# Norm vectors spread by TensorE, expert retrieval for two heads at a time, side work billed by VectorE time, gMLP first in the mixer

## The chip, the cores and the metric

The kernel runs on one core of a Trainium2 chip. The metric is the device time of one execution in microseconds (us); lower is better. The five engines named here are TensorE (PE), VectorE (DVE), ScalarE (ACT), GpSimd (POOL) and SyncE (SP). SP issues the plain transfers, POOL the indirect ones.

## The reference

Two layers act on 256 tokens of width 1024 (two blocks of 128 tokens, b = 0 and 1). An input layer norm comes first. Each layer has a mixer and a channel mixer:

```python
mix = _mixer(h, ...)                     # one projection in, GLA heads | gMLP gate, one projection out
h = _layer_norm(ALPHA * h + mix, ln1_g, ln1_b)
ffn = _peer(h, wq, k1, k2, u_tab, v_tab)
h = _layer_norm(ALPHA * h + ffn, ln2_g, ln2_b)
```

The GLA half is gated linear attention in four heads, in chunks of 64, then an RMS norm and a multiplication by `silu(r)`. The gMLP half is `u * (W LN(v) + b)` with `u` and `v` after a gelu, the layer norm having its own two vectors of 512. `_peer` takes, for each token and each of 8 heads, the best 16 of 128 scores in two halves, then the best 16 of the sums of the two, which name 16 experts out of 16384. Each of the 128 chosen experts of a token (8 heads times 16) adds `gate * gelu(u_e . x) * v_e`; `u_e` and `v_e` are rows of 1024 floats.

## The kernel before, in words

**The main loop** (L785 to L811). There are four passes of K = 128 iterations: layer 0 block 0, layer 0 block 1, layer 1 block 0, layer 1 block 1. In an iteration POOL gathers for one expert slot the `u` and `v` rows of 128 tokens (L730, 128 rows of 8 KB, 1.05 MB), DVE forms the dot products with `h` (`dot`, L737), ACT turns them into a diagonal matrix (`weigh`, L743 to L746), and PE adds the weighted `v` rows to two accumulators (L795). Seven buffers `uv` hold gathered rows (UVBUFS), and gathers are issued up to five ahead (AHEAD). A buffer is free for the next gather when its L795 products are done.

**The side work.** While the experts of one block are gathered, the other block is prepared: generator `side` (L752) runs the residual and norm (`residual_block`, `norm_rest`), the mixer (`front`, L281) and the queries (`ask`, L688). It advances at every `yield`. In each iteration `debt` grows by PACE (0.7, 0.64, 0.64, 0.5 by pass) and one step is run for each whole unit (L807 to L811), so a step counts 1 whatever it costs. What is left of a side at the end of its pass is run at once (L803). Program order on PE, ACT and DVE is the order written; SP and POOL take their work as the scheduler sets it.

**The weights.** `front` and `ask` take 45 chunks of 512 KB for each block and layer through `Feed` (L48): SP loads a chunk into one of four buffers `raw`, ACT makes its high part (`split_hi`, L127), DVE the low part (`split_lo`, L132), PE multiplies by both.

**The mixer.** `front` projects the gates, keys and queries (5 chunks), then runs `attention()` and `tokens()` side by side in rounds (L482). `tokens()` projects v, r, sv and su, four chunks each. Only after both have ended come gelu of su, the spatial gate (L488 to L507), and the output projection over 8 chunks (`out`, L494).

**The queries.** `ask` works in rounds: each round starts one of 16 queries (two for each head) and moves the earlier ones a step: projection, copy, sum, product with the keys, copy, `top16` (L603). After the eighth query of a group of HH = 4 heads, `retrieve` (L626) picks the experts of the four heads in six further steps. Before the main loop the whole of block 0's input norm and `front` runs, then rounds of `ask` until the first four heads are retrieved (L777); the rest of `ask` belongs to the first side.

**The norm vectors.** `load_vec` (L167) has SP load a vector of 1024 floats from HBM into all 128 partitions (512 KB) in one of two buffers `vec`; the gMLP vectors `lnv` use the same two buffers (L286). The constants `iota` are loaded into a `raw` buffer (L578).

Of the kernel before, what the change touches and what calls it, by code (L numbers as in the profile page):

```python
# [37 lines left out]
VECS = 2  # L38
PACE = (0.7, 0.64, 0.64, 0.5)
HH = 4  # L40
KH = HH * TK

# [43 lines left out]

class Trunk:
    def __init__(self, ctx, tc, a, dbg=None):
# [11 lines left out]
        nc.sync.dma_start(self.h[:, 0], a["x"][0:128, :])  # L100
        self.ident = cp.tile([128, 128], F32, name="ident")
# [59 lines left out]
    def layer_norm(self, y, g, b):  # L161
        nc = self.nc
        mv, rs = self.norm_stats(y)
        nc.vector.scalar_tensor_tensor(y, y, mv[:, 0:1], g, op0=OP.subtract, op1=OP.mult)
        nc.vector.scalar_tensor_tensor(y, y, rs, b, op0=OP.mult, op1=OP.add)

    def load_vec(self, vec, pool):  # L167
        r = pool.tile([128, D], F32, name="vec", tag="vec", bufs=VECS)
        self.nc.sync.dma_start(r, vec.to_broadcast([128, D]))
        return r  # L170

    def transpose_quarter(self, src, q, xh, xl, later):
# [3 lines left out]
        for i in range(4):  # L176
            dc = q * 4 + i
            nc.tensor.transpose(p[:, i * 128:(i + 1) * 128], src[:, dc * 128:(dc + 1) * 128], self.ident)
# [5 lines left out]
    def wide(self, b, hi, lo):  # L184


        p = self.bank("a")
        v = p[:, :256].rearrange("p (e t) -> p e t", e=2)
# [14 lines left out]
    def norm_sub(self, b, nm, g):  # L203

        for hf in range(2):
            w = slice(hf * 512, (hf + 1) * 512)
            y = self.h[:, b, w]
            self.nc.vector.scalar_tensor_tensor(y, y, nm, g[:, w], op0=OP.add, op1=OP.mult)

    def norm_scale(self, b, hf, rs, be, out, later):  # L210

        nc = self.nc
        w = slice(hf * 512, (hf + 1) * 512)
        y = self.h[:, b, w]
        nc.vector.scalar_tensor_tensor(y, y, rs, be[:, w], op0=OP.mult, op1=OP.add)
        if out is None:
            self.transpose_quarter(self.h[:, b], hf, self.xh[:, b], self.xl[:, b], later)
        else:
            nc.sync.dma_start(out[b * 128:(b + 1) * 128, w], y)

# [5 lines left out]
    def norm_rest(self, b, nm, var, g, be, out):  # L226

        rs = self.pow_half(var)
        self.norm_sub(b, nm, g)
        later = []  # L230
        for hf in range(2):
            self.norm_scale(b, hf, rs, be, out, later)
        for f in later:
            f()

    def bn_norm(self, b, st, g, be, out=None):
# [8 lines left out]
        self.norm_rest(b, nm, t, g, be, out)  # L245
# [35 lines left out]
    def front(self, pp, l, b, feed):  # L281
# [55 lines left out]
        def in_turn(*works):  # L337
# [3 lines left out]
            while works or live:  # L341
# [7 lines left out]
                yield  # L349
# [10 lines left out]
        def attention():  # L360
# [81 lines left out]
            cat, state["uu"] = m2[:, :D], m2[:, D:D + 512]  # L442
            state["cat"] = cat
# [14 lines left out]

        def tokens():
            def bank():  # L460
# [5 lines left out]
                return p  # L466
            p = yield from bank()
            nc.scalar.copy(vv[:, b], p)
            p = yield from bank()
# [3 lines left out]
            p = yield from bank()  # L473
            nc.vector.tensor_tensor(srh, srh, f["gg"].unsqueeze(1).to_broadcast([128, H, 128]), op=OP.mult)
            state["sr"] = sr
            vn = state["vn"] = tile_of("vn", [128, 512])
            nc.scalar.activation(vn, p, AF.Gelu)
            p = yield from bank()
            self.layer_norm(vn, lnv[:, 0], lnv[:, 1])
            state["su"] = p  # L480

        yield from together(attention(), tokens())  # L482
        cat, uu, vn = state["cat"], state["uu"], state["vn"]
        nc.scalar.activation(uu, state["su"], AF.Gelu)
        p = self.bank("b")
        for g in range(4):
            gs = slice(g * 128, (g + 1) * 128)
            nc.tensor.matmul(p[:, gs], lhsT=f["sw"][:, g], rhs=vn[:, gs], start=True, stop=True)  # L488

        g = self.load_vec(a["ln1_g"][l:l + 1], pp)  # L490
        be = self.load_vec(a["ln1_b"][l:l + 1], pp)
        banks = [self.bank("a") for _ in range(2)]

        def out(dc):  # L494
            hi, lo = feed.get()
            for hf in range(2):
                w = slice(hf * 512, (hf + 1) * 512)
                self.mm(banks[hf], [(ch[:, dc], hi[:, w]), (cl[:, dc], hi[:, w]), (ch[:, dc], lo[:, w])], dc == 0,
                        dc == DC - 1)
            feed.split()  # L500
        out(0)
        yield
        for g4 in range(4):
# [3 lines left out]
        out(1)  # L507
        yield
        later = []
        self.transpose_quarter(cat, 1, ch, cl, later)  # L510
        out(2)
        yield
        for w in later:
# [383 lines left out]
```

## Time and profile before

| | us |
|---|---|
| median of 3 runs (1686.33 to 1688.66) | 1688.13 |
| the profiled execution's own time | 1688.3 |
| its span, first to last instruction | 1686.3 |
| DVE busy | 1169.9 |
| PE busy (pipelined, ends modelled) | 1375.3 |
| ACT busy | 772.0 |
| POOL busy | 622.5 |

All rows of the trace are from the profiled execution. A row with "idle before <- X" says how long the engine stood still ahead of that instruction, and what ended it. The transfer rate in a stretch (GB/s) counts all queues. Some instructions overlap the one behind them on the same engine, so the distance between two starts can be a little shorter than the duration.

### The profile page before, as it was taken

How to read it: one execution, taken by the hardware profiler on the slowest of the kernel's cores; microseconds unless marked ns; L12 is line 12 of the kernel's file. 1: busy time of each engine (PE TensorE's matmuls, PEld its weight loads, DVE VectorE, ACT ScalarE, POOL GpSimd, SP SyncE). 2: the span in 40 equal slices, each digit the busy share in tenths (PEclk: the TensorE clock that was granted, in tenths of full speed). 3: DMA queues.
4: the chain of work that ended last, by engine and by line, in shares of the span. 5: the costliest groups of instructions: out<-in, count | busy, mean ns of one | idle time of the engine just before them, and what ended most of it. 6: DMA issues, size and time to landing. Idle time of an engine off the chain costs nothing.

```text
span 1686.3 us, 17419 instructions
## 1 busy us (share of the span) xinstructions
PE 1375.3 (82%) x4448; PEld 727.5 (43%) x4448; DVE 1169.9 (69%) x2638; ACT 772.0 (46%) x2077; POOL 622.5 (37%) x542
## 2 busy tenths in 40 slices
PE   5875699988978798888977799987987877777775
PEld 4764255545633355444643255543652322222221
DVE  4878877666997667666898567766799554444444
ACT  4642376444534466444534456644444333333332
POOL 0001443434335433543335344343334433333331
PEclk9986999998999999998999999999998999999998
DMA  7764999999999999999999999999999999999995
GB/s 261 239 200 146 421 404 418 418 416 419 418 343 402 406 419 418 419 418 419 418 358 390 418 413 418 419 419 419 418 364 351 422 400 421 421 422 421 421 422 240
DMA packets 106406, 649.09 MB, mean 385 GB/s; under 512 B 12066, under 2 KB 12868, under 8 KB 40772
## 3 DMA queue, kind: packets, MB, share of 16 engines
q0 software_dynamic: 73872, 537.49, 77.7%
q1 hardware_dynamic: 32436, 110.50, 17.4%
q8 instruction: 36, 0.59, 0.1%
q14 instruction: 62, 0.51, 0.1%
HBM read 646.90 MB, written 1.05 MB: 384 GB/s over the span
## 4 chain that ended last, share of the span: by engine, by line
DMA 23%; issue 21%; DVE 17%; PE 16%; POOL 13%; ACT 2%; POOLq 1%; DVEq 0%
DMA uv<-uv,eid 23%; POOL uv L730 13%; PE bank_acc L795 9%; DVE junk L737 6%; PE bank_a L138 5%; DVE i L609 1%; DVE wlo L132 1%; DVE v L607 1%; POOLq L730 1%; DVE S L612 1%; DVE pos L609 1%; DVE qp L701 1%; DVE sums L656 1%; ACT whi L127 0%; DVE sc L607 0%
## 5 line engine op out<-in xcount | busy, mean ns | idle before, releaser
L795 PE MATMUL bank_acc<-uv,dg 128*128 128x512 f32 x2048 | 1006.7, 627 | 195.8 <-ACT dg L746 177.2
L730 POOL DMA_INDIRECT uv<-uv,eid x512 | 603.9, 1179 | 922.0 <-PE bank_acc L795 612.4
L737 DVE SCALAR_TENSOR_TENSOR junk<-uv,h 128x1024 f32<-128x1024 f32 x512 | 626.7, 1224 | 440.4 <-DMA uv<-uv,eid 437.2
L795 PEld LDWEIGHTS bank_acc<-uv,dg 128*128 128x128 f32 x2048 | 377.6, 197 | 722.9 <-ACT dg L746 378.6
L743 ACT ACTIVATE dots<-dots 128x1 f32<-128x1 f32 x512 | 103.6, 202 | 656.3 <-DVE junk L737 655.3
L132 DVE TENSOR_TENSOR wlo<-raw,whi 128x1024 fp32r<-128x1024 f32 x180 | 219.2, 1220 | 22.6 <-issue 11.0
L746 ACT ACTIVATE dg<-ident,dots 128x128 f32<-128x128 f32 x512 | 205.6, 402 | 21.8 <-PE bank_acc L795 5.3
L127 ACT CAST whi<-raw 128x1024 fp32r<-128x1024 f32 x180 | 187.3, 1043 | 40.8 <-DMA raw<-wmix 30.4
L744 ACT ACTIVATE dots<-dots,ex 128x1 f32<-128x1 f32 x512 | 150.8, 294 | 16.6
L138 PE MATMUL bank_a<-x,whi 128*128 128x256 f32 x672 | 114.3, 316 | 49.7 <-DVE qp L701 34.5
L138 PE MATMUL bank_a<-whi,x 128*128 128x512 f32 x384 | 134.5, 458 | 1.0 <-ACT whi L127 0.6
L138 PEld LDWEIGHTS bank_a<-x,whi 128*128 128x128 f32 x672 | 93.6, 205 | 71.5 <-DVE qp L701 45.4
L138 PE MATMUL bank_a<-x,wlo 128*128 128x128 f32 x672 | 92.7, 285 | 0.0
L138 PEld LDWEIGHTS bank_a<-x,wlo 128*128 128x128 f32 x672 | 90.9, 209 | 0.0
L138 PEld LDWEIGHTS bank_a<-whi,x 128*128 128x128 f32 x384 | 72.5, 192 | 37.6 <-issue 25.4
L138 PE MATMUL bank_a<-wlo,x 128*128 128x512 f32 x192 | 66.8, 402 | 7.8 <-DVE wlo L132 7.6
L698 ACT COPY f_half<-bank_a 128x128 f32<-128x128 f32 x64 | 16.9, 264 | 69.5 <-PE bank_a L138 60.2
L138 PEld LDWEIGHTS bank_a<-wlo,x 128*128 128x128 f32 x192 | 36.1, 190 | 20.7 <-DVE wlo L132 13.0
L737 DVE DVE_READ_ACCUMULATOR junk<-uv,h 128x1 f32 x512 | 42.1, 82 | 0.0
L704 PEld LDWEIGHTS bank_b<-kt,qp 128*128 128x128 f32 x128 | 24.1, 202 | 39.0 <-issue 21.5
L704 PE MATMUL bank_b<-kt,qp 128*128 128x128 f32 x128 | 27.6, 300 | 14.4 <-DVE qp L701 14.4
L607 DVE MAX8 v<-S 128x8 f32<-128x128 f32 x128 | 37.2, 291 | 2.2
(132 smaller groups left out, 630.5 us busy)
## 6 DMA issues: line engine op xcount, KB each, us to landing
raw<-wmix SPq DMA_DIRECT2D x180, 512.0 KB
uv<-uv,eid POOLq DMA_INDIRECT x512
vec<-ln_g SPq DMA_DIRECT2D x8, 512.0 KB
vec<-ln_b SPq DMA_DIRECT2D x8, 512.0 KB
h<-x SPq DMA_DIRECT2D x2, 512.0 KB
vec<-ln_in_g SPq DMA_DIRECT2D x2, 512.0 KB
vec<-ln_in_b SPq DMA_DIRECT2D x2, 512.0 KB
lnv<-sgu_ln_g SPq DMA_DIRECT2D x4, 256.0 KB
```

Of the source, the lines that this page charges most:

```text
L127: self.nc.scalar.copy(hi, raw)
L132: self.nc.vector.tensor_tensor(lo, raw, hi.bitcast(F32), op=OP.subtract)
L138: self.nc.tensor.matmul(out, lhsT=l, rhs=r, start=start and i == 0, stop=stop and i == n - 1)
L607: nc.vector.max(v[:, r], vals)
L609: nc.vector.max_index(i[:, r], v[:, r], vals)
L704: nc.tensor.matmul(p2, lhsT=q, rhs=kt[:, l, i % 2], start=True, stop=True)
L730: nc.gpsimd.indirect_dma_start(out=uv, out_offset=None, in_=a["uv"], in_offset=bass.IndirectOffsetOnAxis(ap=eid[:, k:k + 1], axis=0), boun ...
L737: nc.vector.scalar_tensor_tensor(junk, uv[:, :D], 1.0, self.h[:, b], op0=OP.mult, op1=OP.mult, accum_out=dots[:, k:k + 1])
L743: nc.scalar.activation(c, c, AF.Gelu)
L744: nc.scalar.mul(c, c, ex[:, k:k + 1])
L746: nc.scalar.mul(dg, self.ident, c)
L795: nc.tensor.matmul(acc[hf], lhsT=dgs[m], rhs=uvs[m][:, D + hf * 512:D + (hf + 1) * 512], start=m % K == 0, stop=m % K == K - 1)
```

## The change

- **Vectors.** One table `vecs` of 16 rows (64 KB) holds all norm vectors and is loaded once. `spread` multiplies a column of the identity, broadcast to 128 columns, with half a row of the table on PE, and so puts that half row on all 128 partitions of a PSUM bank "b". `norm_rest` and the gMLP norm read it there. `load_vec`, `lnv` and the two buffers go.
- **Heads.** HH is 2: `retrieve` runs four times per `ask`, for two heads each, in four steps. The main loop starts once the first two heads are retrieved.
- **Pacing.** Each `yield` names a cost (2.9 for a round of `ask`, 2.3 for a round of attention and tokens, 2.0, 1.3, 1.5 and so on elsewhere, 1.5 where none is named). PACE is 1.65, 1.36, 1.36, 1.5 by pass, and steps are run while `debt` is above 0.
- **Mixer.** `tokens()` takes sv and su first, then v and r. The spatial gate runs beside the later projections (`beside`), and the first half of the output projection (the gMLP rows, OUTS) beside the end of attention.
- **Queries.** Two queries share one PSUM bank "a".
- **Loads.** `iota` gets a tile of its own and comes last of the constants; `x` of block 1 is loaded inside the first side.

```diff
-VECS = 2
-PACE = (0.7, 0.64, 0.64, 0.5)
-HH = 4
+PACE = (1.65, 1.36, 1.36, 1.5)
+OUTS = (4, 5, 6, 7, 0, 1, 2, 3)
+HH = 2
+V_IN, V_LN1, V_LN2, V_SGU, V_LAYER = 0, 2, 4, 6, 5
+def beside(work, other):
+    while True:
+        try:
+            next(work)
+        except StopIteration as e:
+            return e.value
+        next(other, None)
+        yield
         nc.sync.dma_start(self.h[:, 0], a["x"][0:128, :])
+        self.vecs = cp.tile([16, D], F32, name="vecs")
+        nc.sync.dma_start(self.vecs, a["vecs"])
-    def load_vec(self, vec, pool):
-        r = pool.tile([128, D], F32, name="vec", tag="vec", bufs=VECS)
-        self.nc.sync.dma_start(r, vec.to_broadcast([128, D]))
-        return r
+    def spread(self, row, hf=0):
+        p = self.bank("b")
+        self.nc.tensor.matmul(p, lhsT=self.ident[0:16, row:row + 1].to_broadcast([16, 128]),
+                              rhs=self.vecs[:, hf * 512:(hf + 1) * 512], start=True, stop=True)
+        return p
+    def norm_rest(self, b, nm, var, row, out=None):
         rs = self.pow_half(var)
+        gs = [self.spread(row, hf) for hf in range(2)]
+        bs = []
+        y = [self.h[:, b, hf * 512:(hf + 1) * 512] for hf in range(2)]
+        for hf in range(2):
+            nc.vector.scalar_tensor_tensor(y[hf], y[hf], nm, gs[hf], op0=OP.add, op1=OP.mult)
+            bs.append(self.spread(row + 1, hf))
+        yield 1.5
...
-        order += [c + k for c in (C_V, C_R, C_SV, C_SU) for k in range(4)] + [C_OUT + k for k in range(8)]
+        order += [c + k for c in (C_SV, C_SU, C_V, C_R) for k in range(4)] + [C_OUT + k for k in OUTS]
-        lnv = pp.tile([128, 2, 512], F32, name="lnv", tag="vec", bufs=VECS)
-        nc.sync.dma_start(lnv[:, 0], a["sgu_ln_g"][l:l + 1].to_broadcast([128, 512]))
-        nc.sync.dma_start(lnv[:, 1], a["sgu_ln_b"][l:l + 1].to_broadcast([128, 512]))
+            def gating():
+                mv, rs = self.norm_stats(vn)
+                g, be = [self.spread(V_SGU + V_LAYER * l, x) for x in range(2)]
+                yield
+                nc.vector.scalar_tensor_tensor(vn, vn, mv[:, 0:1], g, op0=OP.subtract, op1=OP.mult)
+                nc.vector.scalar_tensor_tensor(vn, vn, rs, be, op0=OP.mult, op1=OP.add)
+                yield
...
+            yield from beside(out(OUTS[:4]), gate)
         yield from together(attention(), tokens())
+        yield from out(OUTS[4:])
+        yield from self.residual_block(banks, b, V_LN1 + V_LAYER * l)
-            r = self.raw()
-            nc.sync.dma_start(r[:, :160], a["iota"])
...
+            r = tile_of("numbers", [128, 160])
+            nc.sync.dma_start(r, a["iota"])
-                yield
-                for h in range(0, HH, 2):
-                    top16(*[(cand[:, x], sc[:, x], pos[:, x]) for x in (h, h + 1)])
-                    yield
+                top16(*[(cand[:, h], sc[:, h], pos[:, h]) for h in range(HH)])
+                yield 2.2
...
                 def query(i):
-                    p = self.wide(b, *feed.get())
+                    if i % 2 == 0:
+                        banks[0] = self.bank("a")
+                    p = self.wide(b, *feed.get(), banks[0][:, i % 2 * 256:(i % 2 + 1) * 256])
...
                     yield from asked
+                    nc.sync.dma_start(self.h[:, 1], a["x"][128:256, :])
                     feed = self.feed_of(0)
+                    yield 0.1
...
                         debt += PACE[min(i // K, 3)]
-                        while debt >= 1:
-                            debt -= 1
-                            if next(work, work) is work:
+                        while debt > 0:
+                            c = next(work, work)
+                            if c is work:
                                 break
+                            debt -= c or 1.5
```

## Rows read from the trace of the kernel before

**Rows 1.** The page: all transfers, and the transfer rate in 40 equal slices.

```profile
DMA packets 106406, 649.09 MB, mean 385 GB/s; under 512 B 12066, under 2 KB 12868, under 8 KB 40772
GB/s 261 239 200 146 421 404 418 418 416 419 418 343 402 406 419 418 419 418 419 418 358 390 418 413 418 419 419 419 418 364 351 422 400 421 421 422 421 421 422 240
```

**Rows 2.** Stretches: window, length, busy us by engine (instructions), PE clock, DMA share, GB/s.

```profile
0.00:157.50 157.50, 108.37 (x594) 94.44 (x594) 118.21 (x306) 75.16 (x127) 6.03 (x16) 0.87 0.61 204
465.00:545.00 80.00, 63.61 (x161) 27.91 (x162) 68.25 (x218) 32.88 (x100) 35.01 (x30) 0.96 0.95 370
855.00:905.00 50.00, 38.63 (x113) 18.43 (x111) 48.07 (x191) 19.47 (x59) 21.67 (x17) 0.97 0.91 341
1240.00:1295.00 55.00, 44.42 (x136) 22.04 (x134) 53.01 (x209) 21.52 (x69) 21.43 (x19) 0.94 0.86 324
1380.00:1655.00 275.00, 217.03 (x438) 73.82 (x436) 135.68 (x220) 98.62 (x330) 107.67 (x109) 1.00 1.01 422
```

**Rows 3.** The transfers of the norm vectors: issues and size.

```profile
vec<-ln_g SPq DMA_DIRECT2D x8, 512.0 KB
lnv<-sgu_ln_g SPq DMA_DIRECT2D x4, 256.0 KB
```

**Rows 4.** Timeline of SP's queue at the start: start, duration, line, transfer.

```profile
15.00 0.33 SPq L579 DMA_DIRECT2D raw<-iota  x1
...
19.81 13.54 SPq L122 DMA_DIRECT2D raw<-wmix  x6
...
70.24 0.33 SPq L169 DMA_DIRECT2D vec<-ln_b  x1
```

**Rows 5.** Timeline of ACT at the start, with idle time before.

```profile
12.67 1.04 ACT L127 CAST whi<-raw 128x1024 fp32r<-128x1024 f32 x1 [10.65 <-DMA raw<-wmix]
...
71.81 0.59 ACT L181 CAST x<-bank_b 128x512 fp32r<-128x512 f32 x1 [4.63 <-PE bank_b L178]
```

**Rows 6.** Timeline of DVE before the first gather.

```profile
10.20 1.41 DVE L208 SCALAR_TENSOR_TENSOR h<-h,nm,vec 128x512 f32<-128x512 f32 x2 [4.20 <-DMA vec<-ln_in_g]
...
108.64 0.29 DVE L607 MAX8 v<-S 128x8 f32<-128x128 f32 x1
...
111.67 0.28 DVE L607 MAX8 v<-S 128x8 f32<-128x128 f32 x1
...
132.94 0.22 DVE L634 CAST k<-i 128x128 f16<-128x128 uint32 x1
...
136.68 0.33 DVE L607 MAX8 sc<-cand 128x8 f32<-128x54 f32 x2
...
138.30 0.28 DVE L607 MAX8 v<-S 128x8 f32<-128x128 f32 x1
...
156.95 0.23 DVE L680 SCALAR_TENSOR_TENSOR eid<-idx 128x64 uint32<-128x64 f32 x1
```

**Rows 7.** The first gather on POOL's timeline.

```profile
157.45 1.12 POOL L730 DMA_INDIRECT uv<-uv,eid  x1 [64.87 <-DVE sums L682]
```

**Rows 8.** Groups of DVE instructions by shape: busy us, mean ns of one, idle before.

```profile
L737 DVE SCALAR_TENSOR_TENSOR junk<-uv,h 128x1024 f32<-128x1024 f32 x512 | 626.7, 1224 | 440.4 <-DMA uv<-uv,eid 437.2
L132 DVE TENSOR_TENSOR wlo<-raw,whi 128x1024 fp32r<-128x1024 f32 x180 | 219.2, 1220 | 22.6 <-issue 11.0 <-ACT whi L127 8.0 <-PE bank_a L138 2.1
L656 DVE TENSOR_TENSOR sums<-prod 128x512 f16<-128x512 f16 x24 | 10.2, 425 | 0.8
L208 DVE SCALAR_TENSOR_TENSOR h<-h,rnm,vec 128x512 f32<-128x512 f32 x12 | 8.4, 746 | 0.0
L666 DVE TENSOR_TENSOR at_least<-pos,lut 128x1024 f16<-128x1024 f16 x8 | 5.5, 693 | 0.3
L526 DVE SCALAR_TENSOR_TENSOR h<-h,bank_a 128x512 f32<-128x512 f32 x8 | 5.2, 683 | 0.0
```

**Rows 9.** Groups of PE: the accumulating products, with mean ns of one.

```profile
L795 PE MATMUL bank_acc<-uv,dg 128*128 128x512 f32 x2048 | 1006.7, 627 | 195.8 <-ACT dg L746 177.2 <-issue 12.9 <-ACT dots L744 5.1
```

**Rows 10.** Waits in 840 to 905 us: engine and line, on what, total us, times, longest.

```profile
PEld bank_a L138 <- DVE qp L701: 5.8, 4, 2.0
```

More of the change, by code (lines that the diff above doesn't have):

```diff
@@ L83, in together @@
                 works.remove(w)
-        yield
+        yield 2.3
 class Trunk:
@@ L244, in bn_norm @@
         nc.vector.tensor_scalar(nm, mv[:, 0:1], -1.0, None, op0=OP.mult)
-        self.norm_rest(b, nm, t, g, be, out)
+        yield from self.norm_rest(b, nm, t, row, out)
     def dump(self, name, ap):
@@ L457, in front, with out @@
         ch, cl = self.xh[:, other], self.xl[:, other]
+        banks = []
+        def out(dcs):
+            if not banks:
+                banks.extend(self.bank("a") for _ in range(2))
+            for dc in dcs:
+                hi, lo = feed.get()
+                for hf in range(2):
+                    w = slice(hf * 512, (hf + 1) * 512)
+                    self.mm(banks[hf], [(ch[:, dc], hi[:, w]), (cl[:, dc], hi[:, w]), (ch[:, dc], lo[:, w])],
+                            dc == OUTS[0], dc == OUTS[-1])
+                feed.split()
+                yield 1.3
         def tokens():
@@ L472, in tokens, with residual_block @@
             srh = sr.rearrange("p (h c) -> p h c", h=H)
-            p = yield from bank()
             nc.vector.tensor_tensor(srh, srh, f["gg"].unsqueeze(1).to_broadcast([128, H, 128]), op=OP.mult)
             state["sr"] = sr
[L476 to L480, printed above, removed]
-        yield from together(attention(), tokens())
[L483 to L503, printed above, removed]
-            gs = slice(g4 * 128, (g4 + 1) * 128)
-            nc.vector.scalar_tensor_tensor(cat[:, 512 + g4 * 128:640 + g4 * 128], p[:, gs], f["sb"][:, g4:g4 + 1],
-                                           uu[:, gs], op0=OP.add, op1=OP.mult)
[L507 to L513, printed above, removed]
-            w()
-        for dc in range(3, DC):
-            out(dc)
-            yield
-        yield from self.residual_block(banks, b, g, be)
-    def residual_block(self, banks, b, g, be):
+            yield from beside(out(OUTS[:4]), gate)
+        yield from together(attention(), tokens())
+        yield from out(OUTS[4:])
+        yield from self.residual_block(banks, b, V_LN1 + V_LAYER * l)
+    def residual_block(self, banks, b, row):
         nc, sm = self.nc, self.sm
@@ L554, in input_block, with output_block @@
             self.nc.vector.bn_stats(st[:, i], self.h[:, b, i * 512:(i + 1) * 512])
-        yield
-        self.bn_norm(b, st, g, be)
-        yield
-    def output_block(self, banks, b, g, be):
+        yield 1.3
+        yield from self.bn_norm(b, st, V_IN)
+    def output_block(self, banks, b, row):
         nc = self.nc
@@ L566, in output_block @@
             nc.vector.bn_stats(st[:, hf], hs)
-        yield
-        self.bn_norm(b, st, g, be, self.a["out"])
-        yield
+        yield 2.6
+        yield from self.bn_norm(b, st, row, self.a["out"])
     def run(self):
@@ L867, in pack @@
     wm[:, C_WQ:C_WQ + 16] = feat(f["peer_wq"])
+    vecs = np.zeros((16, D), np.float32)
+    vecs[0:2] = f["ln_in_g"].reshape(D), f["ln_in_b"].reshape(D)
+    for l in range(L):
+        vecs[2 + 5 * l:7 + 5 * l] = (f["ln1_g"][l], f["ln1_b"][l], f["ln2_g"][l], f["ln2_b"][l],
+                                     np.concatenate([f["sgu_ln_g"][l], f["sgu_ln_b"][l]]))
     uv = np.concatenate([f["peer_u"].reshape(L * NK * NK, D), f["peer_v"].reshape(L * NK * NK, D)], 1)
@@ L870, in pack @@
         "x": cc(f["x"].reshape(T, D)),
-        "ln_in_g": cc(f["ln_in_g"].reshape(1, D)), "ln_in_b": cc(f["ln_in_b"].reshape(1, D)),
+        "vecs": vecs,
         "wmix": wm, "uv": uv,
```

118 lines of the change are left out of this document (56 added, 62 removed).

## The prediction

> **What bounds the kernel now.** I read the page's rate in slices first: after the fourth slice nearly every slice moves 416 to 422 GB/s [rows 1]. Then the stretches: with no side work the rate is 422 [rows 2], so the kernel is bound by transfers wherever it stands near 420, and I take 419 for the plateau. Away from it there are two kinds of stretch. Up to 157.5 us no gather runs and the rate is 204 [rows 2]: the first gather waits for VectorE's expert numbers [rows 6, 7]. And at the end of each side, where `ask` runs, the rate falls to 370, 341 and 324 while VectorE is busy 68 of 80, 48 of 50 and 53 of 55 us [rows 2]: there VectorE bounds. Those three lose (419-370)/419 x 80 = 9.4 us, 9.3 us and 12.5 us: 31 us.
>
> So span = first gather + bytes left / 419 + losses. Before it: 204 GB/s x 157.5 us = 32.1 MB have moved, 649.1 - 32.1 = 617.0 MB are left [rows 1, 2], which is 1472.6 us, and 1686.3 - 157.5 - 1472.6 = 56 us are losses: the 31 us, and 25 us for filling the queue, small dips and the tail behind the last gather. I work out each term anew.
>
> **Bytes.** The vector loads that go are 20 of 512 KB (`ln_g` and `ln_b` eight each, `ln_in_g` and `ln_in_b` two each) and 8 of 256 KB [rows 3]: 10.5 + 2.1 = 12.6 MB, for a table of 0.07 MB. Before the first gather fall `ln_in_g` and `ln_in_b`, the first layer's `ln1` pair and its `lnv` (2.6 MB), and block 1's `x` (0.5 MB), which moves behind it. Before the first gather 29.0 MB remain, in all 636.6, so 607.6 MB or 1450.1 us are left: -22.5 us. Bounds: 0, if the loads ran in gaps of the gathers, and -30, all 12.6 MB. At 416 to 422 there are no gaps outside `ask`, so -22.5. The Trainium skill, "DMA: Bandwidth & Descriptors", section Bandwidth, says that HBM to SBUF transfers are held to about 358 GB/s for each core; by that these 9.4 MB would be worth 26 us. The trace's 422 [rows 2] contradicts it, and the row decides.
>
> **First gather: two heads instead of four.** From one query's `top16` to the next a round takes 111.67 - 108.64 = 3.03 us, all on VectorE [rows 6]. Retrieval starts four rounds earlier: 12.1 us. Then from its start to `eid` it took 156.95 - 132.94 = 24.0 us, interleaved with the other queries [rows 6]. What retrieving costs: choosing 16 of 54 for two heads is 138.30 - 136.68 = 1.62 us; five products of 1024 halves at 0.69; three sums over 16 places of about 1.2 each, the first step of each 0.425; and about 2.9 of small steps [rows 6, 8]: 13.2 us for four heads by my sum. For two: 1.62, five at the 0.425 that 512 elements take, three sums of about 1.0, the small steps again nearly as long as before (2.8): 9.5 us. Now it spans three rounds of other queries (9.1) and 9.0 of its own: 18. So 6 us less, in sum -18.
>
> **First gather: the front.** Four waits go. VectorE waited 4.2 us for `ln_in_g` [rows 6], and the first chunk reached ACT only at 12.67 [rows 5], behind 1 MB of vectors: -4. SP's queue stood at `iota`, which needed a `raw` buffer, until 15.0, then issued constants until 19.81 before it could load the fifth chunk [rows 4]: `iota` now needs none, -5. SP stood at `ln_b` until 70.24, behind buffer `vec` [rows 4], and PE, ACT and VectorE stood at the end of attention (ACT 4.6 us, [rows 5]); now the gate is done long before and four output chunks fill that place: -5. The 1.5 MB of vectors inside `front` free the early transfers: -2. In sum -16; bounds 0 (each is replaced by the next wait) and -25 (all stand in full and the gate's own chain goes too). First gather at 157.5 - 18 - 16 = 123.5.
>
> **Losses in `ask`.** This is the price. Four retrievals of 9.5 stand where two of 13.2 did: +11.6 us of VectorE in each `ask`, 46 in all. And they overlap more: with HH = 2 a retrieval runs in every round from 10 to 25. One iteration costs VectorE about 1.25 (the dot product 1.22, [rows 8], and its read-out) and the transfers 1.05 MB / 419 = 2.5 us, a chunk 1.25 more. A round is billed 2.9, so at PACE 1.36 it lies over 2.13 iterations: 5.3 us of transfers, 6.6 with a chunk. VectorE has in rounds 10 to 16: 3.03 + 9.5/4 + 2.66 = 8.1; in 17 to 21, without the split of 1.14, 7.0. With the 4% of idle that the row of 855 to 905 shows (48.07 of 50, [rows 2]) that is 1.8 too much in 7 rounds, 1.9 in 5: 22 us. The same sum for the kernel before (1.56 iterations a round, 1.43 in pass 0, retrieval in rounds 14 to 19 and 22 to 27) gives 16, 16 and 20, where 9.3, 12.5 and 9.4 were lost: gathers already queued hide some 7. So 15 us in each of passes 1 and 2. In pass 0 at 1.65 a round has 1.76 iterations: 2.3 x 7 + 2.4 x 5 + 1.5 = 29, less 7: 22. And the rest of the first `ask`, rounds 14 to 26, now falls inside the gathers: 9 in rounds 14 to 16, where no chunk is left to load, 12 in 17 to 21, 2 after them, 23 in all; with hardly a queue built, say 16. In sum 68 against 31: +37.
>
> Against that, PE stood in `ask` until the sum `qp` of the query two before had freed its bank: 5.8 us in one end stretch [rows 10], and products that free `uv` buffers stood behind it. With two queries in a bank the wait is for the third before. I take half of 5.8 in four stretches, some 10, as longer cover: +27. The Trainium skill, "Perfetto Trace Analysis", section Optimizing Tensor Performance, says that independent groups of products should rotate through different PSUM banks, so that emptying one overlaps the next; by it the pair of queries in one bank gives that credit back, and the time would be 10 us longer. No row of before has two queries in a bank.
>
> **What costs nothing.** 48 spreads (ten norms of four, four gates of two), each of two PE instructions at no more than 0.63 [rows 9]: 60 us, 13 a pass; PE has 217 of 275 us busy even without side work [rows 2], but transfers bound there. If that cover goes it is up to +13 a pass. A product read from PSUM costs VectorE 0.683, from SBUF 0.746 [rows 8]: -3 to 0 us in all. The gate's spreads meet attention's four banks "b" in block 1: PE waits there for VectorE, by one round of it, about 4 us; what queues behind is L795 and thus the next gather. Gathers up to five ahead are 12 us of transfers and hide it; without them +4 in two passes. PACE: I count 197 of cost in pass 0 (119 iterations at 1.65) and 160 in passes 1 and 2 (117 at 1.36), so no side is run off at the end. Block 1's `x` is ordered on SP ahead of its use; if late, some 5 us, behind the same queue.
>
> **Sum.** 123.5 + 1450.1 + 56 + 27 = 1657 us of span. The profiled execution took 2.0 more than its span (1688.3 against 1686.3) and agrees with the median, 1688.13, so I predict 1659.
>
> **Rivals.**
> *The queue hides the retrievals* (for it: only 31 of 52 us of surplus were lost before; against: VectorE's 96% in those stretches): losses as before, 123.5 + 1450.1 + 56 + 2 = 1632.
> *The front stays as long* (for it: VectorE is busy 118 of 157.5 us [rows 2], so a freed wait meets the next; against: the waits above end in transfers and in SP's order): first gather at 139.5, 1675.
> *VectorE bounds every `ask`, slower.* Place: rounds 10 to 21 of five stretches. If nothing queued hides and VectorE has 10% of gaps, the surplus is 2.3 us in each of those 12 rounds, 28 in each of passes 1 and 2, 36 at the end of pass 0, 27 at its start: 119 against 31, +88, so 1720. It decides from +56 on, where the 34 of the earlier start and the 22 of bytes are eaten. For it: 46 us more work on the engine that bounds there; against: it needs about twice the surplus that the rows give.
> *Both gains in full* (front -25, nothing lost): 1623.
>
> **How the numbers follow.** Forecast 0.47 (own range 1643 to 1671), hidden retrievals 0.21, front as long 0.13, slower 0.11, both in full 0.08. The range 1626 to 1692 leaves out the last, and most of the slower case. Within 0.2% (3.4 us, what a measurement tells from no change) there is only the edge between cases: 0.03; slower 0.11, faster 0.86.
>
> **What would show it.** No `vec` or `lnv` transfers and some 637 MB; the first gather between 112 and 140 us; no stand of SP near 15 and 70 us; the plateau at 419 again. In the stretches of `ask` rates of 320 to 360 GB/s with VectorE over 95%, longer than before, and such a stretch right behind the first gather. I am wrong in mechanism if the rate falls in `front` instead (spreads, banks), if a side is run off at a pass's end, or if `ask` keeps 415.

## The result, and the profile after

The changed kernel takes 1695.67 us (median of 17 runs, 1690.1 to 1705.8) against 1685.63 us before: a ratio of 1.006, with an interval of 1.0044 to 1.0076. It is slower by 0.6%, where 1659 was forecast. The profiled execution has a span of 1690.7 us.

The page of after, its transfers and its rate in 40 equal slices, to be laid beside [rows 1]:

```profile
GB/s 234 224 143 300 347 390 396 416 417 419 404 330 364 392 418 391 419 419 419 396 353 386 402 399 363 418 419 419 419 320 361 409 372 421 422 421 422 421 421 255
DMA packets 102409, 636.60 MB, mean 377 GB/s; under 512 B 11634, under 2 KB 12436, under 8 KB 36772
```

The bytes fell as reckoned, 649.1 to 636.6 MB, and the plateau is the old one. But the rate now falls in more slices, and not only where `ask` ends. The windows of after, with the columns of [rows 2], show which:

```profile
0.00:139.00 139.00, 115.37 (x551) 92.44 (x551) 100.20 (x233) 71.72 (x115) 6.08 (x15) 0.88 0.58 192
139.00:235.00 96.00, 72.59 (x203) 36.41 (x201) 85.82 (x298) 42.64 (x114) 38.47 (x33) 0.86 0.95 362
450.00:540.00 90.00, 69.41 (x210) 34.68 (x211) 83.90 (x309) 41.32 (x118) 31.37 (x28) 0.91 0.90 344
830.00:930.00 100.00, 78.78 (x233) 39.46 (x233) 92.86 (x326) 47.06 (x135) 37.36 (x34) 0.91 0.94 367
1025.00:1050.00 25.00, 17.98 (x42) 8.25 (x41) 15.11 (x27) 8.99 (x26) 6.85 (x6) 0.80 0.82 324
1230.00:1330.00 100.00, 77.73 (x234) 38.91 (x235) 93.26 (x325) 46.80 (x134) 38.05 (x34) 0.93 0.90 348
1360.00:1380.00 20.00, 20.00 (x35) 8.17 (x34) 10.12 (x16) 5.06 (x18) 6.97 (x7) 0.73 0.83 317
1380.00:1655.00 275.00, 218.74 (x442) 74.59 (x440) 135.67 (x220) 98.74 (x330) 109.78 (x112) 1.00 1.01 421
```

Two kinds of loss are to be seen here; each is (419 less the rate) / 419 of its length. In the four stretches of `ask` VectorE is busy 89 to 93% and 13.1, 16.1, 12.4 and 16.9 us are lost, 58.5 in all. At 1025 and 1360 VectorE has 40 to 50% of its time free, and the rate falls all the same: 5.7 and 4.9 us. The same two places lost 0 and 2.1 us before (419 GB/s there in the first, 374 in the second). There are six such short stretches, three at the mixer's gate (381, 361 and 324 GB/s at 275 to 300, 635 to 655 and 1025 to 1050) and three at the start of a pass (380, 337 and 317 at 560 to 590, 960 to 980 and 1360 to 1380); by the same reckoning they lose 22.3 us together, 4.5 before.

The first gather, on POOL's timeline of after ([rows 7] before):

```profile
139.06 1.12 POOL L726 DMA_INDIRECT uv<-uv,eid  x1 [48.50 <-DVE sums L676]
```

So 192 GB/s x 139.06 us = 26.7 MB have moved by then, 609.9 MB are left, 1455.6 us at 419, and 1690.7 - 139.1 - 1455.6 = 96 us are losses. The miss of 34 us of span is thus 15.6 in the first gather, 5.5 in the bytes left behind it, and 13 in losses.

What a stretch at the gate is made of is read from the timelines of after at 1024 to 1042. PE (start, duration, line, tiles, count, and in brackets the idle time before and what ended it):

```profile
1031.97 2.07 PE L179 MATMUL bank_b<-vecs,ident 16*128 16x512 f32 x2 [5.96 <-DVE f_at L408]
1035.10 2.07 PE L179 MATMUL bank_b<-vecs,ident 16*128 16x512 f32 x2 [1.06 <-DVE f_vn L488]
1037.10 5.07 PE L791 MATMUL bank_acc<-uv,dg 128*128 128x512 f32 x8
```

DVE:

```profile
1026.38 1.23 DVE L733 SCALAR_TENSOR_TENSOR junk<-uv,h 128x1024 f32<-128x1024 f32 x1 [0.33 <-DMA uv<-uv,eid]
...
1030.23 1.23 DVE L733 SCALAR_TENSOR_TENSOR junk<-uv,h 128x1024 f32<-128x1024 f32 x1 [2.61 <-DMA uv<-uv,eid]
...
1031.49 0.42 DVE L408 TENSOR_TENSOR f_at<-bank_b,ident 128x256 f32<-128x256 f32 x1
...
1034.30 0.74 DVE L488 SCALAR_TENSOR_TENSOR f_vn<-f_vn,bnmv,bank_b 128x512 f32<-128x512 f32 x1
```

POOL:

```profile
1026.92 1.59 POOL L726 DMA_INDIRECT uv<-uv,eid  x1 [0.23 <-issue]
1040.72 1.00 POOL L726 DMA_INDIRECT uv<-uv,eid  x1 [12.21 <-PE bank_acc L791]
```

A spread (L179) needs a bank "b". The bank is held by attention until VectorE has read it at L408, and L408 stands on VectorE behind a dot product that waits 2.61 us for its own gather. PE takes its products in order, so it stands; and behind the spread stand the eight products L791, which free the `uv` buffers. What they read had long been ready: ACT ended the second of their two diagonal matrices (L742) at 1028.61, and they began at 1037.10. No gather is issued for 13.8 us. PE came out of the idle time at a granted clock of 0.50 (1031 to 1037), the level of 1.2 GHz, at which two instructions of a spread take 2.07 us; in the kernel with spreads alone (before_spread, below) two took 1.02 at a granted clock of 1.00, the level of 2.4 GHz:

```profile
775.84 1.02 PE L173 MATMUL bank_b<-vecs,ident 16*128 16x512 f32 x2
```

### The profile page after: what moved, and what is told of

Same layout as the page of the kernel before. It is cut to its first block, busy times and chain, and to the rows that moved or that the text cites. A ratio compares the mean times of both kernels' runs of the same rounds, so it can differ in the third digit from the quotient of the medians.

```text
span 1690.7 us, 17829 instructions
## 1 busy us (share of the span) xinstructions
PE 1430.4 (85%) x4544; PEld 749.1 (44%) x4544; DVE 1204.0 (71%) x2898; ACT 794.7 (47%) x2106; POOL 614.1 (36%) x542
## 4 chain that ended last, share of the span: by engine, by line
DVE 28%; DMA 24%; issue 19%; PE 14%; POOL 12%; ACT 2%; POOLq 1%; DVEq 0%; SPq 0%; ACTq 0%
DMA uv<-uv,eid 23%; POOL uv L726 11%; DVE junk L733 10%; PE bank_acc L791 7%; PE bank_a L153 5%; DVE wlo L147 3%; DVE i L605 2%; DVE v L603 2%; PE bank_b L179 1%; DVE S L608 1%; DVE sums L650 1%; POOLq L726 1%; DVE pos L605 1%; DVE sums L651 1%; ACT whi L142 1%
## 5 line engine op out<-in xcount | busy, mean ns | idle before, releaser
L791 PE MATMUL bank_acc<-uv,dg 128*128 128x512 f32 x2048 | 1012.3, 629 | 199.0 <-ACT dg L742 187.7
L726 POOL DMA_INDIRECT uv<-uv,eid x512 | 595.8, 1164 | 917.8 <-PE bank_acc L791 599.1
L791 PEld LDWEIGHTS bank_acc<-uv,dg 128*128 128x128 f32 x2048 | 375.6, 196 | 723.4 <-ACT dg L742 383.9
L147 DVE TENSOR_TENSOR wlo<-raw,whi 128x1024 fp32r<-128x1024 f32 x180 | 218.9, 1219 | 35.0 <-issue 16.9
L742 ACT ACTIVATE dg<-ident,dots 128x128 f32<-128x128 f32 x512 | 205.6, 402 | 38.5 <-PE bank_acc L791 21.9
L153 PE MATMUL bank_a<-x,whi 128*128 128x256 f32 x672 | 118.9, 325 | 9.3 <-ACT f_half L694 6.1
L153 PEld LDWEIGHTS bank_a<-x,whi 128*128 128x128 f32 x672 | 98.2, 213 | 24.6 <-issue 9.8
L179 PE MATMUL bank_b<-vecs,ident 16*128 16x512 f32 x96 | 58.9, 752 | 23.8 <-DVE f_at L408 11.9
L179 PEld LDWEIGHTS bank_b<-vecs,ident 16*128 16x128 f32 x96 | 19.5, 219 | 55.2 <-issue 30.2
```

The costliest lines, as they stand in the source:

```text
L147: self.nc.vector.tensor_tensor(lo, raw, hi.bitcast(F32), op=OP.subtract)
L153: self.nc.tensor.matmul(out, lhsT=l, rhs=r, start=start and i == 0, stop=stop and i == n - 1)
L179: self.nc.tensor.matmul(p, lhsT=self.ident[0:16, row:row + 1].to_broadcast([16, 128]), rhs=self.vecs[:, hf * 512:(hf + 1) * 512], start=Tr ...
L726: nc.gpsimd.indirect_dma_start(out=uv, out_offset=None, in_=a["uv"], in_offset=bass.IndirectOffsetOnAxis(ap=eid[:, k:k + 1], axis=0), boun ...
L742: nc.scalar.mul(dg, self.ident, c)
L791: nc.tensor.matmul(acc[hf], lhsT=dgs[m], rhs=uvs[m][:, D + hf * 512:D + (hf + 1) * 512], start=m % K == 0, stop=m % K == K - 1)
```

## The experiments

**The gate two turns later.** Theory A: the gate's spreads stand in PE before banks that attention holds.

```
 def gating():
+    yield
+    yield
     mv, rs = self.norm_stats(vn)
```

> The changed kernel, with the gMLP gate's norm and its two spreads begun two rounds of attention later. Theory A (PE stands at the gate's second spread until VectorE has read attention's bank, and the gathers' products stand behind it): the three stretches in the mixer that lost 2.3, 2.8 and 5.7 us keep under 3 us together, span about 8 us shorter, ratio to the kernel before 1.000 to 1.003. Rival (the stretches come from the new order of the projections, or from VectorE): they stay, ratio 1.006.

Measured: 1687.13 us, ratio 0.9999 (0.9987 to 1.0011), 0.6% less than after. The windows of this kernel at the two gates that had 324 and 361 GB/s:

```profile
1025.00:1050.00 25.00, 24.59 (x79) 13.31 (x79) 21.48 (x42) 15.84 (x37) 11.95 (x10) 1.00 1.01 417
630.00:655.00 25.00, 24.12 (x79) 13.21 (x78) 21.37 (x39) 14.45 (x34) 12.23 (x9) 1.00 1.02 418
```

The stretches are gone, and the clock is full; the third gate, 381 GB/s in after, has 417 at 275 to 300. (These windows are of an execution of 1679.4 us, 7.8 below the median, so they are no measure of the whole gain.) Over the whole of after, PE waited ahead of a spread for attention's step L408 as follows; in this kernel the wait does not occur:

```profile
PE bank_b L179 <- DVE f_at L408: 11.9, 3, 6.0
```

(In us: the total, how often, the longest.) The gate's spreads cost next to nothing when the banks are free on their turn. Theory A stands.

**The residual's spreads in the first step.** The same theory for the starts of the passes.

```
+        vecs = [self.spread(row + x, hf) for x in range(2) for hf in range(2)]
         for hf in range(2):
-            junk = self.bank("b")
+            junk = self.ring.tile([128, 512], F32, name="square", ...)
...      (norm_rest takes these vecs and issues no spreads of its own)
```

> The changed kernel with all four spreads of a residual norm issued in its first step, ahead of the wait for its statistics (the squares go to SBUF, so that four banks are free). Theory E (at a pass's start PE's spreads and its waits stand between the accumulating products, when no gather is queued): the three low stretches there (2.8, 3.9, 4.9 us) lose half, span 4 to 7 us shorter, ratio 1.001 to 1.004. Rival (they come from the accumulator's bank and PE's clock alone): unchanged, ratio 1.006.

Measured: 1689.07 us, ratio 1.0009 (0.9997 to 1.0022). Windows of it at the three starts:

```profile
560.00:600.00 40.00, 39.35 (x151) 21.58 (x150) 30.03 (x54) 27.55 (x67) 17.71 (x14) 0.96 1.01 418
960.00:1000.00 40.00, 38.69 (x158) 22.74 (x158) 28.61 (x48) 25.24 (x63) 17.97 (x15) 1.00 1.02 419
1360.00:1380.00 20.00, 19.91 (x39) 7.83 (x37) 10.78 (x18) 6.54 (x24) 9.04 (x8) 0.85 0.79 307
```

Two of three are gone. The third belongs to the output block, which this edit does not touch, and it stays here. The edit also takes the squares out of the banks "b"; what that alone does is not parted from the earlier spreads.

**The old order of the mixer, with spreads.**

```
-        order += [c + k for c in (C_SV, C_SU, C_V, C_R) ...
+        order += [c + k for c in (C_V, C_R, C_SV, C_SU) ...
         (and the gate behind the gates of the attention, as before)
```

> The changed kernel with the mixer's old order (v, r, sv, su, gate after attention, output chunks 0 to 7), all else as changed. Theory C (the front at the start is held by VectorE's and PE's work, not by the waits that went): first gather within 4 us of 139.1; and, by theory A, no low stretches in the mixer, as the spreads come when attention's banks are free: ratio about 1.000. Rival (gMLP first shortened the front, and something else held it): first gather at 144 us or later, ratio 1.006 or more.

Measured: 1692.96 us, ratio 1.0027 (1.0011 to 1.0044), first gather at 141.97. The new order of the mixer is worth at most 3 us of the front, as theory C expected. The low stretches at the gates go with it, as theory A expected: the rate is 417, 418 and 419 GB/s at 242 to 380, 590 to 830 and 990 to 1230 us, where after has 411, 414 and 409. The ratio is 1.0027 and not about 1.000: the pass starts stay (202 at 970 to 980), and there is a new one of 325 at 380 to 400, where the four spreads of the mixer's norm stand in a row on PE (eight instructions from 382.73).

**The spreads alone, put into the kernel before.** The vector loads go, the table and the spreads come, everything else stays.

```
-        g = self.load_vec(a["ln1_g"][l:l + 1], pp)
...
+        gs = [self.spread(row, hf) for hf in range(2)]
```

> The kernel before with only the vectors changed: spread by PE from the table, four heads, old pacing, old mixer order. Theory D (the bytes are worth their 22 to 25 us, and the spreads cost only where PE stands ahead of the gathers' products, at the residuals): 636.6 MB, span 1662 to 1672, ratio 0.986 to 0.992. Rival (the spreads' waits eat the bytes wherever they stand): ratio 0.997 or more.

Measured: 1702.99 us, ratio 1.0091 (1.0078 to 1.0104). The expectation failed and its rival came: 12.5 MB less were moved, and it became slower. The bytes did give what they were expected to: 28.6 MB had moved at the first gather, and the 608.0 MB left take 1451 us at 419, 22 less than before. But the losses are 1698.3 - 160.0 - 1451 = 87 us for the 56 of before. The first gather is at 159.98, so the front, with vector transfers out and spreads in, did not become shorter. Timeline of PE of this kernel at one residual:

```profile
778.70 1.12 PE L173 MATMUL bank_b<-vecs,ident 16*128 16x512 f32 x2
780.71 0.66 PE L183 MATMUL bank_b<-ident,h 128*128 128x128 f32 x4 [0.90 <-DVE h L222]
781.30 1.40 PE L173 MATMUL bank_b<-vecs,ident 16*128 16x512 f32 x2
783.54 1.11 PE L183 MATMUL bank_b<-ident,h 128*128 128x128 f32 x4 [0.84 <-DVE h L222]
784.45 7.50 PE L794 MATMUL bank_acc<-uv,dg 128*128 128x512 f32 x12
```

A spread, VectorE's step that reads it, the transposes of what that step wrote, the next spread: PE and VectorE wait for each other in turn, and twelve accumulating products queue behind. At 780 to 790 the rate is 165 GB/s, 420 in before. At the two neighbouring norms of this kind it is 321 (580 to 590) and 359 (970 to 990), 421 and 407 in before.

**Four heads in the changed kernel, two in the old one.** Theory B: four retrievals cost VectorE more than two.

```
 after:   -HH = 2    before:  -HH = 4
          +HH = 4             +HH = 2
```

> The changed kernel with HH = 4: one retrieval of four steps for four heads. Theory B (retrieving for two heads at a time costs more in the five stretches of the queries, 58 us lost, than the earlier first gather gives): first gather back at about 157 us (+18), those stretches lose 15 to 25 us, span 15 to 22 us shorter, ratio 0.993 to 0.998. Rival (the earlier first gather is worth its 18 us, and the losses come from the new pacing): losses stay near 50, span about 10 to 18 us longer, ratio 1.012 to 1.017.

> The kernel before with HH = 2 alone. Theory B (retrieving for two heads brings the first gather 18 us forward and costs more than that where the queries run): first gather at 139 to 140 us, losses in the five stretches of the queries 31 -> 65 us or more, ratio 1.006 to 1.015. Rival (the earlier start is worth its time and the losses came from the new pacing): losses under 45, ratio 0.992 to 0.998.

Measured: four heads in after 1687.2 us, ratio 1.0006 (0.9989 to 1.0023), first gather 151.14; two heads in before 1716.32 us, ratio 1.0171 (1.0157 to 1.0186), first gather 141.94. Windows of before with two heads at the three ends of `ask`:

```profile
450.00:540.00 90.00, 67.59 (x231) 37.03 (x230) 85.57 (x341) 39.83 (x106) 26.89 (x24) 0.92 0.87 330
850.00:930.00 80.00, 61.79 (x187) 32.22 (x188) 75.86 (x297) 33.61 (x94) 24.45 (x23) 0.89 0.86 325
1260.00:1340.00 80.00, 59.80 (x181) 29.21 (x180) 75.27 (x293) 33.61 (x97) 29.21 (x25) 0.95 0.82 302
```

VectorE is busy 94 to 95% there, and 19, 18 and 22 us are lost where [rows 2] had 9.4, 9.3 and 12.5. In after the three ends fall from 45 us to 25 with four heads (378, 375 and 353 GB/s over 80, 60 and 70 us), while the short stretches at the gates and the pass starts grew by some 8 us, which took part of the gain back. Two heads alone, on the old bill, cost 1.7%: the earlier start of 15.5 us does not pay for it. Theory B stands, with a larger price than expected in before and a smaller gain in after: 1.0006 lies outside the 0.993 to 0.998 that it gave.

**SP's two waits taken away in before.** Theory C: they are replaced.

```
-            r = self.raw()
+            r = tile_of("numbers", [128, 160])
...      (iota last of the constants, x of block 1 inside the first side)
-VECS = 2
+VECS = 3
```

> The kernel before with SP's stands alone taken away: iota in a tile of its own, last of the constants, a third buffer vec, x of block 1 loaded in the first side. Theory C (each wait that goes from the front is replaced by VectorE's and PE's own work): SP no longer stands at 15 and 70 us, first gather at 154 to 157.5 us, ratio 0.998 to 1.000. Rival (the waits stand in the sum, as predicted: 5 us each): first gather at 147 to 150 us, ratio 0.994 to 0.996.

Measured: 1685.7 us, ratio 0.9994 (0.9985 to 1.0003), first gather at 153.60. SP's queue no longer stands for `iota` or for `ln_b` [rows 4], and 3.9 us come of it, not 10. The fifth chunk is ordered at 18.70, 1.1 us earlier than before: the other constants now fill SP's queue ahead of it.

**Head groups of 2, 2, 4 in the first pass and 4, 4 in the others, with the gate late (best1); with the residual's spreads early as well (best2).**

```
-HH = 2
+HH = 4      (the size of the tiles)
+GROUPS = ((2, 2, 4), (4, 4), (4, 4), (4, 4))
...
```

> The changed kernel with the gate two rounds later, and heads retrieved in groups of 2, 2, 4 for the first block and 4, 4 for the rest. Theories A and B together: first gather at 135 to 136 us, its following stretch loses under 10 us, the three ends of the queries 25 to 30 us in all, none in the mixer: span 1658 to 1668, ratio 0.985 to 0.991. Rival (what the groups of four save is lost again at the residuals or in the front): ratio 0.996 or more.

> best1 with one more part of after moved: the four residual spreads of a norm are issued in the step before the squares, and the squares go to a tile in SBUF and not to a bank. Theory E (PE, in order, stands at the residual's spreads for banks and the next gather's release stands behind it): the low stretches at the three pass starts, 6.0, 7.7 and 3.1 us in best1 by bytes, fall to some 5 in all as they did in after_res_early, so 8 to 12 us off best1's span of 1665.2: 1653 to 1658, ratio to before 0.980 to 0.984. Rival (the stretch at a pass start is the change of pass itself, the queue that is refilled): it stays, ratio 0.986 to 0.989.

Measured: best1 1666.95 us, ratio 0.9876 (0.9859 to 0.9893); best2 1653.92 us, ratio 0.9799 (0.9786 to 0.9813). The second start of a pass, its window and rows of PE's timeline, best1 first, then best2 (there the pass begins some 11 us earlier):

```profile
940.00:960.00 20.00, 19.78 (x35) 8.39 (x36) 11.27 (x23) 7.12 (x21) 3.94 (x4) 0.60 0.70 281
940.22 3.75 PE L804 MATMUL bank_acc<-uv,dg 128*128 128x512 f32 x4 [3.80 <-issue]
943.90 7.19 PE L180 MATMUL bank_b<-vecs,ident 16*128 16x512 f32 x8
```

```profile
925.00:945.00 20.00, 20.00 (x64) 10.11 (x64) 17.41 (x31) 12.18 (x31) 8.27 (x7) 0.83 1.01 418
925.24 4.84 PE L180 MATMUL bank_b<-vecs,ident 16*128 16x512 f32 x8
```

In best2 the spreads fill the time in which PE has nothing else to do. In best1 PE stands 3.80 us, comes out at a granted clock of 0.50 (940 to 955), and the eight instructions of the four spreads take 7.19 us ahead of the products that free `uv` buffers. Both count as busy, but it is 35 instructions against 64.

All three pass starts are gone in best2, a little more than expected. The third has no spread of a residual in it, only those of the output block, which the edit leaves where they were. Their rows, after first, then best2:

```profile
1358.98 7.19 PE L179 MATMUL bank_b<-vecs,ident 16*128 16x512 f32 x8
```

```profile
1316.81 3.88 PE L180 MATMUL bank_b<-vecs,ident 16*128 16x512 f32 x8
```

The granted clock was 0.50 in the first and 0.95 in the second, though PE had stood about as long shortly before (2.64 and 2.92 us). So the third start went because PE's clock did not fall there; why it did not is open.

**The bill of the steps.** Theory F: the loss in `ask` comes from a bill of 2.9 for every round, whatever it holds.

```
-                    yield 2.9
+                    yield cost or 0.01      (the sum of what the round's steps returned:
                                              1.2 a split, 1.75 a top16, a retrieval's
                                              steps by the number of their heads)
-        yield 2.3
+        yield 2.1                            (a round of attention and tokens)
-                yield 2.0
+                yield 1.6                    (a round of the mixer's first projections)
-PACE = (1.65, 1.36, 1.36, 1.5)
+PACE = (1.63, 1.31, 1.31, 1.5)               (best3, best4: 1.57, 1.24, 1.24, 1.5)
```

> best2 with the side's steps billed nearer to the VectorE time that they cost (a query's round of ask by what it holds, 1.75 and more where a retrieval or a split stands in it, in place of 2.9 for each; a retrieval's steps by the number of its heads), and PACE 1.57, 1.24, 1.24, 1.5 so that a side still fills its pass. Theory F (VectorE bounds at the ends of ask because rounds that hold a retrieval are billed like those that hold none, so the surplus stands in a row): the ends of ask, 9.8, 7 and 12.5 us in best1, fall to a half: ratio 0.972 to 0.980. Rival (the total of VectorE's work in a pass bounds, and a better spread over the rounds moves the low stretch elsewhere or leaves a side to be run off at the end of a pass): no change against best2, 0.980 to 0.985, or a new low stretch before 1380 us.

> The changed kernel with its side steps billed by what they cost VectorE (a round of ask by what it holds in place of 2.9 for each) and PACE 1.63, 1.31, 1.31, 1.5, which ends each side some four iterations before its pass does; two heads, the gate and the residual stay as in after. Theory F (the surplus of the ends of ask comes from rounds billed alike): the stretches at the ends of ask, 16.1, 12.4 and 16.9 us in after, fall to 8 to 11 each, so 12 to 20 us off after's 1695.7: 1676 to 1684, ratio to before 0.993 to 0.999. Rival (four retrievals are too much VectorE work whatever their spacing): 1690 to 1697, ratio 1.002 to 1.007.

> The kernel before, with nothing changed but the bill of the steps of ask: a round counts what it holds of VectorE time (1.2 us a split, 1.75 a top16 of a query, 1 to 3.2 for each step of a retrieval), divided by 2.2 us, in place of one for each round; PACE stays at 0.7 and 0.64, by which the sides still end 4 to 7 iterations before their passes. If the even bill of a round is what costs in ask, whatever else is changed, the stretches at the ends of ask, 9.4, 9.3 and 12.5 us in before, fall to some 2 to 5 each: 1665 to 1672 us, ratio 0.988 to 0.993; then the change, paced alike (0.980), is worth about 1% of its own. Rival (it was two heads that asked for the other bill, and before's two retrievals of four heads lie far enough apart): 0.997 to 1.000, and nearly all of the 2% of after_paced belongs to the change.

In before_paced only the steps of `ask` are billed anew, each by these costs divided by 2.2, and PACE stays.

Measured: the changed kernel with this bill and PACE and nothing else (after_paced) 1653.0 us, ratio 0.9797 (0.9776 to 0.9819); the kernel before with its own `ask` billed in this way (before_paced) 1670.04 us, ratio 0.991 (0.9896 to 0.9923); best2 with the bill (best3) 1639.01 us, ratio 0.9699 (0.9678 to 0.972). Windows of after_paced:

```profile
140.00:240.00 100.00, 80.86 (x208) 39.91 (x208) 89.67 (x310) 44.36 (x120) 43.23 (x36) 0.83 0.96 381
440.00:545.00 105.00, 84.49 (x252) 40.92 (x253) 97.71 (x332) 50.55 (x152) 44.03 (x39) 0.97 1.00 405
830.00:930.00 100.00, 81.56 (x211) 36.09 (x209) 83.98 (x268) 44.67 (x133) 49.10 (x40) 0.95 1.01 414
1190.00:1250.00 60.00, 54.87 (x188) 29.29 (x188) 54.01 (x164) 28.44 (x90) 27.36 (x23) 0.95 0.98 392
```

By the same sum these lose 9.1, 3.5, 1.2 and 3.9 us, 18 where after lost 58.5, with the same four retrievals of two heads. The expectation of 12 to 20 us was too small by half: 43 came. So the work of four retrievals in a pass was not too much for VectorE, as the rival had it; it was crowded.

The edit does two things at once, though. It spreads the work evenly over the rounds, and it gives `ask` more of the pass. From the first sum `qp` of a query to the last `eid`, counted in VectorE's dot products, `ask` lies over 38, 47 and 47 iterations in after and 48, 61 and 61 in after_paced (35, 38 and 38 in before, 47, 51 and 51 in before_paced), time that had been left at the end of the pass or that the lower bills of the mixer set free. How much comes from each is not parted: no run has an even bill that is merely higher.

And the kernel before has the same fault, in a smaller measure, 0.9%: in before_paced the rate at its three ends of `ask` is 379, 335 and 389 GB/s over 40, 30 and 70 us, 15 us lost for the 31 of [rows 2]. Paced in much the same way, the change is worth 0.9797 / 0.991 = 0.989, some 1.1% faster; with its own bill it is 0.6% slower.

**The table and the identity loaded first (best4, on best3).**

```
-        nc.sync.dma_start(self.h[:, 0], a["x"][0:128, :])
         nc.sync.dma_start(self.vecs, a["vecs"])
         nc.sync.dma_start(self.ident, a["ident"])
+        nc.sync.dma_start(self.h[:, 0], a["x"][0:128, :])
```

> best3 with the small table and the identity loaded ahead of the first block of x, and nothing else. In after PE waited 8.43 us for the identity before the first spread, and VectorE's first norm step came at 10.51 us. If that wait sets the front, the first gather comes 1.5 to 2.5 us earlier (133.1 to about 131) and the ratio is 0.968 to 0.970; if x and the first weights are the later end, as all waits of the front have been replaced so far, the first gather stays within 1 us of 133.1.

Measured: 1639.16 us, ratio 0.9709 (0.969 to 0.9728), the same as best3. PE waits 3.13 us for the identity, 7.80 in best3, and ACT has the first half of `x` 2.3 us earlier (13.71 for 16.04); but the first gather, on POOL's timeline of best3 and then of best4, is not earlier:

```profile
133.08 1.12 POOL L741 DMA_INDIRECT uv<-uv,eid  x1 [47.69 <-DVE sums L684]
```

```profile
135.55 1.12 POOL L741 DMA_INDIRECT uv<-uv,eid  x1 [47.76 <-DVE sums L684]
```

The first gather varies between executions: after and after_paced have the same order of instructions up to it, and it comes at 139.06 and 141.94. before and before_paced, with one order too, have it at 157.45 and 154.62. Differences of some 3 us there decide nothing, and of the 3.9 us of before_sp_free little is certain. best3 is the fastest of these kernels, 3.0% below the kernel before.

## Why the prediction was wrong

**Bytes: right, with a small slip.** 636.6 MB as forecast. But 26.7 MB and not 29.0 moved before the first gather, so more was left behind it: 5.5 us.

**Two heads: right.** 18 us were forecast, 12.1 for the earlier start and 6 for the shorter retrieval. VectorE's rows of after show it, laid beside 108.64, 132.94 and 156.95 in [rows 6]: the first `top16` of a query, the start of the retrieval, its end.

```profile
109.12 0.29 DVE L603 MAX8 v<-S 128x8 f32<-128x128 f32 x1
121.28 0.19 DVE L630 CAST k<-i 128x64 f16<-128x64 uint32 x1
138.59 0.19 DVE L674 SCALAR_TENSOR_TENSOR eid<-idx 128x32 uint32<-128x32 f32 x1
```

The retrieval begins 11.7 us earlier and takes 17.3 us for 24.0. The runs that change the heads alone gave 12.1 us (after with four) and 15.5 (before with two), with the variation of some 3 us in them.

**The front: this step failed.** The prediction let four waits go for 16 us, and named replacement by the next wait as its lower bound of 0 and as a rival of 0.13. That is what happened: the first `top16` came at 109.12, 108.64 before, so the front gave nothing that stands out of the variation, and the first gather came at 139.06, the rival's 139.5. before_hh2 says the same: with the old front and two heads its first gather is at 141.94. Two of the waits alone gave 3.9 us, not 10 (before_sp_free); the vectors' transfers, with spreads in their place, gave nothing (before_spread, 159.98); PE's wait for the identity gave nothing (best4). At 80 to 130 us PE is busy 44.08 of 50 us at a granted clock of 0.75 in after, 37.31 at 0.86 in before, and the transfers move 148 for 200 GB/s. So the loads were not what held the front; which chain of PE, ACT and VectorE does hold it, these runs do not part.

**"What costs nothing": this step failed; it and the front turned the sign.** The prediction saw that the gate's spreads meet attention's banks, and that the products L795 and the next gather stand behind them, and then let the queued gathers hide it. The rows show a gap of 13.8 us between gathers and 5.7 us of lost transfer: the queue hid a part. It also let the spreads' PE time (60 us forecast, 58.9 measured) vanish beside free PE time. At the gates they cost as waits: not the two instructions, but what PE's order puts behind them. At the starts of the passes they cost as time too: eight instructions in a row, 7.19 us at the lower clock, ahead of the products on which the next gather waits. The losses in the six stretches rose by 18 us; the prediction's bounds were 13 a pass for the spreads' time and 4 in two passes for the gate. The Trainium skill, "PSUM — Partial Sum Buffer", section Engine vs sequencer instructions, says that matmuls start and complete in program order, while a weight load may overlap those in flight; the trace agrees: the eight accumulating products at 1037.10 start when the second spread ends, and they touch no bank "b". One reading of rows was wrong here, without weight in the sum: 0.683 and 0.746 [rows 8] are two different steps (L526, L208), and the step of L208 itself, reading bank "b" in after (L227), took 0.742 for 0.746, so a product read from PSUM gave nothing.

**Losses in `ask`: right in size, and not the whole truth.** Forecast 58 (31 + 27), measured 58.5. By stretch 16, 22, 15 and 15 were forecast, less 10 for the credit, and 13.1, 16.1, 12.4 and 16.9 came, so the agreement to half a microsecond is in part luck. The sum by rounds took the bill of 2.9 as it stands; after_paced shows that with another bill the same work loses 18. The wait for which the credit of two queries in a bank was taken went: PE's weight loads waited 45.4 us for `qp` at `ask`'s and the mixer's products in before, and the waits of that group name it no more in after. That this gave the 10 us is not shown, as no run has that part of the change alone. By the Trainium skill, "Perfetto Trace Analysis", section Optimizing Tensor Performance, independent groups of products should rotate through different PSUM banks, so two in one bank should give that back; here PE's wait is gone and ACT has a longer one. The rows of the copy `f_half`, before and then after, show it (busy, mean ns, idle before and what ended it):

```profile
L698 ACT COPY f_half<-bank_a 128x128 f32<-128x128 f32 x64 | 16.9, 264 | 69.5 <-PE bank_a L138 60.2 <-DVE v L607 5.0 <-DVE cand L612 2.4
```

```profile
L694 ACT COPY f_half<-bank_a 128x128 f32<-128x128 f32 x64 | 17.0, 265 | 113.6 <-DVE qp L697 109.1 <-PE bank_a L153 4.5
```

What that costs is open: after_paced has 111.4 us of the same wait and loses only 18 us in `ask`.

**The rivals.** The kernel is slower, but not by the slower rival, which needed 119 us of losses in `ask`. It is the forecast's `ask`, the rival's front, and a cost that stood among the things that cost nothing.

## What to carry to other kernels

A small instruction on an engine that runs in order costs what stands behind it while it waits, not only its own time: before counting it as hidden, look at who holds its buffer at that moment and what is queued next. When work is interleaved by a bill, check the bill against the measured time of each step, and how much of the pass the work is given, before the work itself is changed: here the two together were worth 0.9% in the old kernel and 2.6% in the new one; the change, with its own bill, cost 0.6%. And a wait that is removed in a stage where several engines take turns is worth nothing until the next one has been looked up.

## What the runs showed of the hardware

PE came out of idle time at the lower level of its clock: 0.50 at 1031 to 1037 us of after, when it had stood 5.96 us; 0.50 at 940 to 955 in best1, when it had stood 3.80 us; 0.50 at 1359 to 1366 in after, shortly after 2.64 us. It does not always fall: in best2 PE stood 2.92 us ahead of 1314.49 and the spreads behind ran at 0.95. So a wait of PE in the middle of a bound stretch can be paid twice, once as idle time and once as products at half speed (two spread instructions 2.07 us for 1.02, eight 7.19 for 3.88).
